# Half of the row squares moved to the head, the rest given two products to land, and row factors written to DRAM in runs

## The chip, the cores and the metric

The kernel runs on one core of one Trainium2 chip. The metric is the device time of one execution in microseconds (us). The core has five engines with queues of their own: TensorE (PE, with a separate unit for weight loads, PEld), VectorE (DVE), ScalarE (ACT), GpSimd (POOL) and SyncE (SP). Transfers (DMAs) are issued from the queues of SP, ACT and POOL and run on 16 shared DMA engines.

## The reference, cut to what matters

One layer of an encoder block is applied to two batches with shared weights, 512 and 256 tokens, together T = 768 rows of D = 2048 numbers in float32:

```
h = RMSNorm(x) * g;  z = h @ w_in           # columns: fourier 1024 | q 1024 | k 256 | v 256
of = fourier_mix(z fourier);  oa = windowed attention(q, k, v)
x = x + [RMSNorm(of) | RMSNorm(oa)] @ w_out
x = x + relu(RMSNorm(x) @ w_up)**2 @ w_down
y = RMSNorm(x)
```

RMSNorm needs one factor for each row of x, rsqrt(mean(x * x) + eps). The kernel does not scale x by it before the first product: it multiplies gains into x, computes z without the row factor, and applies the factor later to the columns of the transposed z (tile `rb`) or to the attention's probabilities (tile `r0`).

## The kernel before, in words

All large products are made of three float32r matmuls: each operand is split into a high part (a copy to float32r on ACT) and a low part (the rest, a subtraction on DVE), and high x high, high x low and low x high are summed in PSUM. So every operand costs one ACT and one DVE instruction ahead of PE.

The change lies in the first 170 us, which have three stages.

1. **The head** (inside the pool `xp`): x transposed is loaded by SP in chunks of one or two blocks of 128 of the 2048 columns (`chunks`, `load_x`), alternating with the weights of v (`load_wv`, four tiles `wv` with the tag `raw`). `prepare(c)` scales a chunk by the gains and splits it; `v_term` makes 36 matmuls of 256 columns for two blocks (line 425). The last chunk also makes the high and low parts of the first two weight pieces (`high7`, `low7`). Then come `xsum` (differences of x blocks on DVE) and `v_keep`, which copies the six results of v out of PSUM.
2. **The 28 products** (pool `hq`, the loop over n): the Fourier columns of z by a seven-product scheme (`names7`) with four weight pieces each. Iteration n issues, in the order of the code: x operand parts (`high_at`), the weight sums, `high7(n + 3)`, `low7(n + 2)`, further x parts (`low_at`), `product7(n)` (24 matmuls of 384 columns, line 276), the copy or addition of the results before (`out7`), and the load of the weights for n + 5. SP, ACT and DVE keep this written order, as PE does everywhere. Among the `low_at` steps are `first_load` and `first_split`, which fetch the first x block again into the tile `d7` and split it for the next stage.
3. **The rest of z** (line 789, 20 weight pieces), with the Fourier transform beside it; `fold` multiplies by `rb` at line 550.

The rows' squares stand in stage 2. From n = 10 on, POOL loads x by rows in 24 pieces of 512 numbers (`row_load`, line 482) into the tile `d7`, three at a time, and ACT squares and sums each in place (`row_square`, line 486) into one column of `ssq`. A piece can be loaded only when ACT is through with the one that was there. At n = 20 `row_norms` sums the columns (DVE), makes the factor `r0` [128, 6] (POOL, lines 98 and 101), writes it to DRAM (line 491) and reads it back as a row spread over all partitions, `rb` (line 492):

```
nc.gpsimd.dma_start(r0_d[0].rearrange("(m p) -> p m", p=P), r0[:])
nc.gpsimd.dma_start(rb[:], r0_d[0].partition_broadcast(P))
```

The tile pool `hq` uses the memory of `xp` after it; its weight tiles `wr` come first, as the tiles `raw` do in `xp`. PSUM has four buffers with the tag `ps` and four with `f`, shared by v, the products and the next stage.

Of the kernel before, what the change touches and what calls it, by code (L numbers as in the profile page):

```python
# [40 lines left out]
def hybrid_encoder(ctx: ExitStack, tc: tile.TileContext, a: dict):  # L41
# [83 lines left out]

    gall = cpool.tile([P, 3 * NK], F32, tag="gall", name="gall")
    g0, gm, gcat = (gall[:, i * NK : (i + 1) * NK] for i in range(3))
    r0_d = dpool.tile([1, T], F32, tag="r0d", name="r0d")
    ss0, r0, r1, r2, rm, ry = (stat(x) for x in ("ss0", "r0", "r1", "r2", "rm", "ry"))
    ssx, ssy = stat("ssx", NM * 4), stat("ssy", NM * 4)  # L130
    ssq = ssx

    def transpose4(ps, src):

# [62 lines left out]
    with ExitStack() as ph:  # L197
# [135 lines left out]

        def first_load(e):
            fx["d"] = hq["p"].tile([P, 4, HALF], F32, tag="d7", name="d7")[:]
            nc.sync.dma_start(fx["d"], a["x_t"][:, 0, 4 * e : 4 * e + 4, :])

        def first_split(e):
            for i in range(4):
# [26 lines left out]
            step(high_at, 20 + e, lambda e=e: xhigh(h0, b21, e))  # L366
            step(low_at, 20 + e, lambda e=e: xlow(l0, b21, h0, e))
        step(low_at, 22, first_block)
        step(low_at, 22, lambda: first_load(0))
        for e in range(2):  # L370
            step(low_at, 24 + 2 * e, lambda e=e: first_split(e))
            if e == 0:
# [3 lines left out]
        with tc.tile_pool(name="xp", bufs=1, reuse_waits="tile") as xp, tc.manual_schedule(  # L376
            engines={mybir.EngineType.SP, mybir.EngineType.Activation, mybir.EngineType.DVE}
        ):

            wv = [xp.tile([P, 4, 256], F32, tag="raw", name="raw", bufs=4) for _ in range(4)]  # L380
            whl = [[wpool.tile([P, 4, 256], F32R, tag=t, name=t, bufs=4) for t in ("wh", "wl")] for _ in range(4)]
            flat = xs[1][:].rearrange("p o k t -> p (o k t)").rearrange("p (s o t) -> p s o t", s=8, o=2)
            vt = xp.tile([P, 4, 2, HALF], F32R, tag="vt", name="vt")
            room = [flat[:, 0:4], flat[:, 4:8], vt[:]]
            chunks = [(0, 1), (1, 1), (2, 2), (4, 2), (6, 2), (8, 2), (10, 2), (12, 2), (14, 2)]
            homes = [(0, 0), (0, 1), (0, 2), (1, 0), (1, 2), (2, 0), (0, 0), (1, 0), (2, 0)]
            xhl = {}

            def load_x(k0, n):
                for t in range(2):  # L390
                    nc.sync.dma_start(xr[k0 // 8][t][:, k0 % 8 : k0 % 8 + n, :], a["x_t"][:, t, k0 : k0 + n, :])

            def load_wv(k0, n, queue=nc.sync):
                queue.dma_start(wv[k0 // 4][:, k0 % 4 : k0 % 4 + n, :], w_in[9][:, k0 : k0 + n, :])

            def prepare(c):

                k0, n = chunks[c]
                r, s0 = homes[c]
                ks = slice(k0 % 8, k0 % 8 + n)  # L400
                raw = [xr[k0 // 8][t][:, ks, :] for t in range(2)]
                rows = [room[r][:, s0 + i * n : s0 + i * n + n] for i in range(2 if k0 >= 8 else 1)]
                if k0 < 8:
                    parts = [[xs[0][:, o, ks, :] for o in range(2)]]
                else:
                    parts = []
                parts += [[x[:, :, o, :] for o in range(2)] for x in rows]
                xhl[c] = parts
                w, wk = k0 // 4, slice(k0 % 4, k0 % 4 + n)
                wh, wl = (x[:, wk, :] for x in whl[w])  # L410
                for i in range(n):
                    nc.scalar.activation(raw[0][:, i], raw[0][:, i], AF.Copy, scale=g0[:, k0 + i : k0 + i + 1])
                gb = g0[:, k0 : k0 + n].rearrange("p (k o) -> p k o", o=1).to_broadcast([P, n, HALF])
                nc.vector.tensor_tensor(out=raw[1], in0=raw[1], in1=gb, op=ALU.mult)
                split(wh, wl, wv[w][:, wk, :])
                for t in range(2):
                    split(*parts[t], raw[t])

            pv = [pp.tile([P, 512], F32, tag="f" if m < 4 else "ps", bufs=4, name="pv") for m in range(NM)]

            def v_term(c, m, term, i):
                k0, n = chunks[c]
                l, r = ((0, 0), (0, 1), (1, 0))[term]
                k = k0 + i
                nc.tensor.matmul(  # L425
                    pv[m][:, :256], xhl[c][m // 3][l][:, i, m % 3 * P : (m % 3 + 1) * P], whl[k // 4][r][:, k % 4, :],
                    start=(k == 0 and term == 0), stop=(k == NK - 1 and term == 2),
                )

            def v_keep(m):  # L430
                split(vhl[:, m, :, 0, :], vhl[:, m, :, 1, :], pv[m][:, :256].rearrange("p (g d) -> p g d", g=NKV))

            pw = pp.tile([P, 512], F32, tag="ps", bufs=4, name="pw")
            for i in range(9):
                nc.tensor.matmul(pw[:, :P], ones[:], ones[:], start=True, stop=True)
            nc.scalar.activation(mhalf[:, 7:8], mhalf[:, 7:8], AF.Copy)
            nc.scalar.dma_start(gall[:], a["gains"])
            load_wv(0, 1)
            load_x(*chunks[0])
            load_wv(1, 1)  # L440
            load_x(*chunks[1])
            load_wv(2, 2)
            load_x(*chunks[2])
            load_wv(4, 4)
            load_x(*chunks[3])
            load_x(*chunks[4])
            load_wv(8, 4)
            load_x(*chunks[5])
            load_x(*chunks[6])
            load_wv(12, 4)  # L450
            load_x(*chunks[7])
            load_x(*chunks[8])
            load7(0)
            load7(1)
            for c, (k0, n) in enumerate(chunks):
                prepare(c)
                if c == 5:
                    nc.scalar.dma_start(ident[:], a["c_ident"])
                if c + 1 < len(chunks):
                    for term in range(3):  # L460
                        for m in range(NM):
                            for i in range(n):
                                v_term(c, m, term, i)
                else:
                    for n2 in range(2):
                        high7(n2)
                        low7(n2)
                    for m in range(NM):
                        for term in range(3):
                            for i in range(n):  # L470
                                v_term(c, m, term, i)
            for n in range(2):
                xsum(b11, b12, b11, n)
            for m in range(NM):
                v_keep(m)

        def row_load(i):
            m, h = divmod(i, 4)
            if i == 0:
                raw7["x"] = hq["p"].tile([P, 4, HALF], F32, tag="d7", name="d7")[:].rearrange("p k t -> p (k t)")  # L480
            xt = raw7["x"][:, i % 3 * 512 : (i % 3 + 1) * 512]
            nc.gpsimd.dma_start(xt, x_rows(m)[:, h * 512 : (h + 1) * 512])  # L482
# [5 lines left out]
        def row_norms():  # L488
            nc.vector.tensor_reduce(out=ss0[:], in_=ssq[:].rearrange("p (m h) -> p m h", h=4), op=ALU.add, axis=AX.X)
            rsqrt_of(r0[:], ss0[:], D, NM, nc.gpsimd)  # L490
            nc.gpsimd.dma_start(r0_d[0].rearrange("(m p) -> p m", p=P), r0[:])
            nc.gpsimd.dma_start(rb[:], r0_d[0].partition_broadcast(P))

        with tc.tile_pool(name="hq", bufs=1, reuse_waits="tile") as hq["p"], tc.manual_schedule(
            engines={mybir.EngineType.SP, mybir.EngineType.Activation, mybir.EngineType.DVE}
        ):
            for n in range(2, 5):
                load7(n)
            high7(2)
            for n in range(NP7):  # L500
                for fn in high_at.get(n, ()):
                    fn()
                sum7(n + 3)
                high7(n + 3)
                low7(n + 2)
                for fn in low_at.get(n, ()):
                    fn()
                product7(n)
                out7(n - 1)
                load7(n + 5)  # L510
                if n == 10:
                    for i in range(3):
                        row_load(i)
                for i in range(3 * n - 36, 3 * n - 33):
                    if 0 <= i < 4 * NM:
                        row_square(i)
                for i in range(3 * n - 33, 3 * n - 30):
                    if 3 <= i < 4 * NM:
                        row_load(i)
                if n == 20:  # L520
                    row_norms()
            out7(NP7 - 1)
            out7(-1)

# [1291 lines left out]
```

## Time and profile before

| | |
|---|---|
| time, median of 3 runs | 2591.98 us (2587.20 to 2593.43) |
| the profiled execution | 2586.95 us, its span 2585.1 us |
| PE busy | 2565.6 us, 99% of the span |
| DVE, ACT, POOL busy | 1795.9, 1122.6, 252.9 us |
| mean granted clock of TensorE | 0.997 |

The span is the time between the first and the last instruction that the profiler shows. In the rows of a timeline stand the start, the duration, the engine, the line, the operation, the tiles written and read, and in brackets the idle time before it with what ended it. In the rows of waits stand who waited for whom, the us in total, how often, and the longest. In the rows of windows stand, for each stretch, the busy us of PE, PEld, DVE, ACT and POOL with their counts, the granted clock of TensorE, the busy share of the DMA engines and GB/s.

### The profile page before, as it was taken

Reading aid. Unit: us, or ns where it says so; the run is one execution under the profiler, and the core shown is the slowest. Engines: PE = TensorE matmul, PEld = TensorE weight load, DVE = VectorE, ACT = ScalarE, POOL = GpSimd, SP = SyncE. Lnnn points to the kernel's source line nnn. Section 1 sums busy time; section 2 is a strip of 40 time slices with the busy share of each in tenths; the row PEclk is TensorE's granted clock in tenths of the full one; section 3 lists DMA queues with packets and bytes.
Section 4 is the critical chain, followed back from the end, with each engine's and each line's share of the span. In section 5 each row is a group of like instructions: output and inputs, shape, how many; then the busy total and the mean of one; then the engine's idle time right before and its main releaser. Section 6 shows DMA issues by size and latency. Waiting matters only on the chain.

```text
span 2585.1 us, 34796 instructions
## 1 busy us (share of the span) xinstructions
PE 2565.6 (99%) x13462; PEld 2347.8 (91%) x13462; DVE 1795.9 (69%) x2212; ACT 1122.6 (43%) x1627; POOL 252.9 (10%) x355
## 2 busy tenths in 40 slices
PE   9999999999999999999999999999999999999998
PEld 9999998888899999999999999988888888888887
DVE  8756558787565555556777787667776766777687
ACT  6644337674333333334444544433333333333335
POOL 0112322222201011000000000110000000000000
PEclk9999999999999999999999999999999999999999
DMA  7673467455664445456666666775543662554364
GB/s 262 223 206 128 130 218 224 138 151 197 220 198 162 153 170 186 153 188 241 217 220 225 228 212 207 260 297 177 181 155 112 217 232 81 175 186 157 100 212 149
DMA packets 259479, 487.84 MB, mean 189 GB/s; under 512 B 20656, under 2 KB 147376, under 8 KB 259056
## 3 DMA queue, kind: packets, MB, share of 16 engines
q1 hardware_dynamic: 187104, 320.20, 38.7%
q10 hardware_dynamic: 58512, 112.05, 11.4%
q0 software_dynamic: 13696, 53.36, 6.0%
q8 instruction: 106, 1.74, 0.3%
q14 instruction: 61, 0.50, 0.1%
HBM read 365.99 MB, written 119.54 MB: 188 GB/s over the span
## 4 chain that ended last, share of the span: by engine, by line
PE 94%; DMA 2%; DVE 2%; issue 1%; ACT 1%; POOL 0%; SPq 0%; POOLq 0%; DVEq 0%; ACTq 0%
PE pu L1183 36%; PE pd L1618 35%; PE pm L1036 9%; PE pz L789 5%; PE p L276 2%; PE pv L425 1%; PE o L914 1%; PE s L835 1%; PE t L892 1%; PE ptx L136 0%; DMA d<-in_x_t 0%; PE pe L618 0%; POOL d L482 0%; PE pa L597 0%; DMA zf<-zf 0%
## 5 line engine op out<-in xcount | busy, mean ns | idle before, releaser
L1183 PE MATMUL pu<-xf,wh 128*128 128x384 f32 x3072 | 780.3, 334 | 0.0
L1183 PEld LDWEIGHTS pu<-xf,wh 128*128 128x128 f32 x3072 | 554.1, 188 | 1.5 <-ACT o L1201 1.3
L1618 PE MATMUL pd<-wh,sh 128*128 128x512 f32 x1332 | 517.7, 389 | 0.0
L1618 PE MATMUL pd<-wl,sh 128*128 128x512 f32 x1332 | 517.7, 389 | 0.0
L1618 PE MATMUL pd<-wh,sl 128*128 128x512 f32 x1332 | 517.5, 389 | 0.0
L1183 PE MATMUL pu<-xf,wl 128*128 128x384 f32 x1536 | 513.1, 334 | 0.0
L1595 ACT ACTIVATE wh<-rd 128x1024 fp32r<-128x1024 f32 x200 | 202.5, 1054 | 522.1 <-PE pd L1618 413.3
L1605 DVE TENSOR_TENSOR wl<-rd,wh 128x1024 fp32r<-128x1024 f32 x200 | 236.1, 1221 | 226.2 <-ACT wh L1595 225.5
L1163 ACT ACTIVATE wh<-ur 128x1024 fp32r<-128x1024 f32 x160 | 170.1, 1063 | 382.7 <-PE pu L1183 204.9
L1618 PEld LDWEIGHTS pd<-wh,sl 128*128 128x128 f32 x1332 | 249.9, 188 | 52.2 <-DVE sl L1606 0.3
L1618 PEld LDWEIGHTS pd<-wh,sh 128*128 128x128 f32 x1332 | 250.0, 188 | 51.7
L1618 PEld LDWEIGHTS pd<-wl,sh 128*128 128x128 f32 x1332 | 250.0, 188 | 51.7
L1183 PEld LDWEIGHTS pu<-xf,wl 128*128 128x128 f32 x1536 | 288.4, 188 | 0.0
L1169 DVE TENSOR_TENSOR wl<-ur,wh 128x1024 fp32r<-128x1024 f32 x160 | 195.5, 1222 | 76.1 <-ACT wh L1163 76.1
L1204 DVE TENSOR_TENSOR o<-pu,o 128x768 f32<-128x768 f32 x160 | 152.9, 956 | 122.5 <-PE pu L1183 114.9
L1588 DVE TENSOR_TENSOR rd<-rd 128x1024 f32<-128x1024 f32 x112 | 131.7, 1218 | 0.0
L1183 PE MATMUL pu<-xs,wh 128*128 128x384 f32 x512 | 129.9, 334 | 0.0
L1163 ACT ACTIVATE wh<-sx 128x1024 fp32r<-128x1024 f32 x64 | 67.9, 1062 | 130.5 <-PE pu L1183 104.4
L276 PE MATMUL p<-xs,wh 128*128 128x384 f32 x448 | 116.2, 340 | 4.1 <-DVE z L293 3.3
L1606 DVE TENSOR_TENSOR sl<-sr,sh 128x768 fp32r<-128x768 f32 x111 | 105.6, 951 | 0.0
L1169 DVE TENSOR_TENSOR wl<-sx,wh 128x1024 fp32r<-128x1024 f32 x64 | 78.2, 1223 | 23.8 <-ACT wh L1163 23.6
L1183 PEld LDWEIGHTS pu<-xs,wh 128*128 128x128 f32 x512 | 92.5, 188 | 0.0
(283 smaller groups left out, 3856.2 us busy)
## 6 DMA issues: line engine op xcount, KB each, us to landing
rd<-in_w_down SPq DMA_DIRECT2D x176, 512.0 KB, 4.9
ur<-in_w_up SPq DMA_DIRECT2D x128, 512.0 KB, 3.9
sr<-sd SPq DMA_DIRECT2D x95, 384.0 KB, 5.1
pd<-o ACTq DMA_DIRECT2D x60, 384.0 KB, 2.3
o<-pd POOLq DMA_DIRECT2D x60, 384.0 KB, 6.0
sd<-sm ACTq DMA_DIRECT2D x60, 384.0 KB, 2.7
raw<-in_w_in SPq DMA_DIRECT2D x42, 512.0 KB, 4.3
raw<-in_w_out SPq DMA_DIRECT2D x32, 512.0 KB, 4.5
```

Source lines behind the costliest of these rows:

```text
L276: nc.tensor.matmul(ps7[bank, g, r][:, :HALF], l[:, i, r * P : (r + 1) * P], x[:, o, 4 * e + i, :], start=(opens and e == 0 and i == 0 and ...
L789: nc.tensor.matmul(ps[c][s][:, :HALF], w[:, i, cs], whole[j // 2][s][o][:, 4 * (j % 2) + i, :], start=first and n == 0, stop=stop and n == 2,)
L1036: nc.tensor.matmul(ps, l(k), w[:, k % 2, :], start=(k == 0 and n == 0), stop=(k == 7 and n == 2))
L1163: nc.scalar.activation(wh[:], raw[:], AF.Copy)
L1169: nc.vector.tensor_tensor(out=wl[:], in0=raw[:], in1=f32(wh[:]), op=ALU.subtract)
L1183: nc.tensor.matmul(ps[:, t, :HALF], w[:, i, t * P : (t + 1) * P], xb[:, o, i, :], start=(s == first_of[bank] and i == 0 and n == 0), stop= ...
L1204: nc.vector.tensor_tensor(out=o, in0=src, in1=o, op=ALU.add)
L1588: add = lambda x, y, op: nc.vector.tensor_tensor(out=x[:], in0=x[:], in1=y[:], op=op)
L1595: nc.scalar.activation(wh[:], t[:], AF.Copy)
L1605: nc.vector.tensor_tensor(out=wl[:], in0=t[:], in1=f32(wh[:]), op=ALU.subtract)
L1606: nc.vector.tensor_tensor(out=sl[:], in0=sr[:], in1=f32(sh[:]), op=ALU.subtract)
L1618: nc.tensor.matmul(o, l[:, q, ts], w[:, ns], start=(j == j0 and (q, t) == (0, 0)), stop=(j == j1 and (q, t) == (1, 2)),)
```

## The change

- The head: the chunk of blocks 2 and 3 becomes two chunks of one block each, loaded in the order v weights, x, v weights, x.
- Rows 0 to 2 of the six blocks of rows are squared in the head, in six halves of 1024 numbers. POOL loads them into the tiles that held the v weights; ACT squares four ahead of the first high parts of weights and two behind them. The other 12 pieces of 512 stay in the loop: loads at n = 10, 12, 14 and 16, squares at n = 12, 14, 16 and 18. `ssq` is cleared at the start, since only two of its four columns are written for the first three blocks.
- `row_norms` moves from n = 20 to n = 18. At n = 21 PE transposes `r0` to [6, 128]; at n = 24 ACT copies that to SBUF, and POOL writes it to DRAM as six runs of 512 bytes and reads it back spread.
- `first_load` goes from SP's queue to POOL's, and its first call from step 22 to step 20.
- The identity for the transpose is loaded at n = 0, not in the head.

```diff
-    r0_d = dpool.tile([1, T], F32, tag="r0d", name="r0d")
+    r0_d = dpool.tile([NM, P], F32, tag="r0d", name="r0d")
...
+    nc.vector.memset(ssq[:], 0.0)
...
         def first_load(e):
             fx["d"] = hq["p"].tile([P, 4, HALF], F32, tag="d7", name="d7")[:]
-            nc.sync.dma_start(fx["d"], a["x_t"][:, 0, 4 * e : 4 * e + 4, :])
+            nc.gpsimd.dma_start(fx["d"], a["x_t"][:, 0, 4 * e : 4 * e + 4, :])
...
-        step(low_at, 22, lambda: first_load(0))
+        step(low_at, 20, lambda: first_load(0))
...
-            chunks = [(0, 1), (1, 1), (2, 2), (4, 2), (6, 2), (8, 2), (10, 2), (12, 2), (14, 2)]
-            homes = [(0, 0), (0, 1), (0, 2), (1, 0), (1, 2), (2, 0), (0, 0), (1, 0), (2, 0)]
+            chunks = [(0, 1), (1, 1), (2, 1), (3, 1), (4, 2), (6, 2), (8, 2), (10, 2), (12, 2), (14, 2)]
+            homes = [(0, 0), (0, 1), (0, 2), (0, 3), (1, 0), (1, 2), (2, 0), (0, 0), (1, 0), (2, 0)]
...
+            def half_load(i):
+                m, h = divmod(i, 2)
+                halves[i] = xp.tile([P, 4, 256], F32, tag="raw", name="xt", bufs=4)[:].rearrange("p a b -> p (a b)")
+                nc.gpsimd.dma_start(halves[i], x_rows(m)[:, h * 1024 : (h + 1) * 1024])
+
+            def half_square(i):
+                m, h = divmod(i, 2)
+                nc.scalar.activation(halves[i], halves[i], AF.Square, accum_out=ssq[:, 4 * m + h : 4 * m + h + 1])
...
             for c, (k0, n) in enumerate(chunks):
                 prepare(c)
-                if c == 5:
-                    nc.scalar.dma_start(ident[:], a["c_ident"])
+                for i in {6: (0, 1), 8: (2,), 9: (3, 4, 5)}.get(c, ()):
+                    half_load(i)
...
+                    for i in range(4):
+                        half_square(i)
                     for n2 in range(2):
                         high7(n2)
                         low7(n2)
+                    for i in range(4, 6):
+                        half_square(i)
...
-            nc.gpsimd.dma_start(r0_d[0].rearrange("(m p) -> p m", p=P), r0[:])
-            nc.gpsimd.dma_start(rb[:], r0_d[0].partition_broadcast(P))
+
+        def row_turn():
+            pr = raw7["r"] = pp.tile([P, 512], F32, tag="ps", bufs=4, name="pr0")
+            nc.tensor.transpose(pr[:NM, :P], r0[:], ident[:])
+
+        def row_spread():
+            pr = raw7.pop("r")
+            nc.scalar.copy(rb[:NM, :P], pr[:NM, :P])
+            nc.gpsimd.dma_start(r0_d[:], rb[:NM, :P])
+            nc.gpsimd.dma_start(rb[:], r0_d[:].rearrange("m p -> (m p)").partition_broadcast(P))
...
-                if n == 10:
-                    for i in range(3):
+                if n == 0:
+                    nc.scalar.dma_start(ident[:], a["c_ident"])
+                if n in (12, 14, 16, 18):
+                    for i in range(3 * n // 2 - 6, 3 * n // 2 - 3):
+                        row_square(i)
+                if n in (10, 12, 14, 16):
+                    for i in range(3 * n // 2 - 3, 3 * n // 2):
                         row_load(i)
-                for i in range(3 * n - 36, 3 * n - 33):
-                    if 0 <= i < 4 * NM:
-                        row_square(i)
-                for i in range(3 * n - 33, 3 * n - 30):
-                    if 3 <= i < 4 * NM:
-                        row_load(i)
-                if n == 20:
+                if n == 18:
                     row_norms()
+                if n == 21:
+                    row_turn()
+                if n == 24:
+                    row_spread()
```

More of the change, by code (lines that the diff above doesn't have):

```diff
@@ L428, in v_term @@
                 )
+            def half_load(i):
[5 more added lines that the diff above has]
+                nc.scalar.activation(halves[i], halves[i], AF.Square, accum_out=ssq[:, 4 * m + h : 4 * m + h + 1])
+            halves = {}
             def v_keep(m):
@@ L437, in hybrid_encoder @@
             nc.scalar.dma_start(gall[:], a["gains"])
[L438 to L452, printed above, removed]
+            for c in range(4):
+                load_wv(c, 1)
+                load_x(*chunks[c])
+            for c in range(4, 10, 2):
+                load_wv(2 * c - 4, 4)
+                load_x(*chunks[c])
+                load_x(*chunks[c + 1])
             load7(0)
@@ L478, in row_load @@
             m, h = divmod(i, 4)
-            if i == 0:
+            if i == 12:
                 raw7["x"] = hq["p"].tile([P, 4, HALF], F32, tag="d7", name="d7")[:].rearrange("p k t -> p (k t)")
```

## The prediction, made before the changed kernel had run

> **What bounds the kernel now.** I read the page's head and chain first, then who TensorE (PE) waits for, then the clock by windows, then the timeline of the engines where PE waits.
>
> ```profile
> span 2585.1 us, 34796 instructions
> PE 2565.6 (99%) x13462; PEld 2347.8 (91%) x13462; DVE 1795.9 (69%) x2212; ACT 1122.6 (43%) x1627; POOL 252.9 (10%) x355
> ...
> PE p L276 <- DVE z L293: 3.3, 1, 3.3
> PE pv L425 <- ACT xs L69: 1.9, 1, 1.9
> PE p L276 <- DVE wl L261: 1.5, 1, 1.5
> ...
> PE p L276 <- ACT wh L253: 0.8, 1, 0.8
> ...
> 117.20:123.90 6.70, 3.40 (x13) 3.11 (x12) 5.41 (x6) 6.66 (x11) 2.15 (x4) 0.75 0.55 166
> 143.30:151.30 8.00, 5.74 (x22) 5.10 (x22) 7.73 (x8) 6.06 (x8) 4.95 (x3) 0.79 0.66 225
> ...
> 12.16 30.51 PE pv L425 x252
> 42.67 49.77 PE p L276 x287
> ...
> 42.51 0.51 PE L276 MATMUL p<-xs,wh 128*128 128x384 f32 x2
> ...
> 120.86 0.98 PE L276 MATMUL p<-xs,wh 128*128 128x384 f32 x2 [3.30 <-DVE z L293]
> ...
> 168.51 0.34 PE L276 MATMUL p<-xs,wl 128*128 128x384 f32 x1
> 169.48 1.17 PE L789 MATMUL pz<-xf,wh 128*128 128x384 f32 x4 [0.63 <-ACT wh L69]
> ```
>
> PE is busy 99% of the span, so only its few holes can be won; all named ones lie before 170 us. The last number but two of a window row is the granted clock: beside both holes it is 0.75 and 0.79, so a hole costs its width and a slow stretch behind it. The two waits before the second hole, 0.8 and 1.5, and the first, 3.3, are 5.6 us of width. How much in all: unhindered, 287 matmuls of the 28 products (line 276) take 49.77 us, 0.1734 each. The products hold 28 x 24 = 672, thus 116.5 us; they run from 42.51 to 168.68 (the last starts at 168.51), 126.2 us. So **9.7 us are lost inside the products**, of which the clock behind the holes is 9.7 - 5.6, about 2 each; 0.6 more at the entry to the next stage and 1.9 in the head.
>
> Who makes the two holes? The row squares on ScalarE (ACT), whose order is fixed:
>
> ```profile
> 86.63 1.81 POOL L482 DMA_DIRECT2D d<-in_x_prompt  x3 [86.20 <-DVE xs L313]
> ...
> 94.22 0.63 ACT L486 ACTIVATE d<-d 128x512 f32<-128x512 f32 x1
> ...
> 110.05 0.54 POOL L482 DMA_DIRECT2D d<-in_x_prompt  x1 [1.01 <-ACT d L486]
> ...
> 114.27 0.63 ACT L486 ACTIVATE d<-d 128x512 f32<-128x512 f32 x1 [3.56 <-DMA d<-in_x_prompt]
> ...
> 116.99 1.47 ACT L310 ACTIVATE xs<-xr 128x1536 fp32r<-128x1536 f32 x1
> ...
> 118.49 1.76 DVE L313 TENSOR_TENSOR xs<-xr,xs 128x1536 fp32r<-128x1536 f32 x1 [6.52 <-ACT xs L310]
> ...
> 141.34 0.63 ACT L486 ACTIVATE d<-d 128x512 f32<-128x512 f32 x1 [0.34 <-DMA d<-in_x_sample]
> ...
> 143.35 1.04 ACT L253 ACTIVATE wh<-raw 128x1024 fp32r<-128x1024 f32 x1
> ...
> DMA to landing us min/median/max: 3.0/6.0/7.4
> ```
>
> A batch of three loads lands 3.0 to 7.4 us after its issue, but its squares stand one product later, 24 x 0.1734 = 4.16 us. ACT waits at 114.27; behind it stand the split of an x operand (line 310) and VectorE's low half, done at 120.25, just before PE resumes at 120.86. Before the second hole a weight's high part (143.35) stands behind the squares of 141.34. Where a batch had two products, 86.63 to 94.22, no wait is marked.
>
> **The change part by part.** All sums are against the profiled execution, 2586.95 us (span 2585.1 and 1.85 around it). That is 5.0 below the median of the runs, 2591.98, so the forecast for the median is the same difference taken from 2591.98.
>
> *Squares with two products to land.* Only rows 3 to 5 stay in the products: loads at n = 10, 12, 14, 16, squares at 12 to 18. Two products are 8.3 us against 7.4 for the slowest landing. Each batch can only be issued when ACT has squared the one before in the same tile (as at 110.05), some 2 us into its iteration, so ACT may still wait about 1 us; the weights it splits are for a product three ahead, 12 us. Both holes go, with their slow clock: all of the 9.7, unless something else is late. Next late is VectorE's low half, which had 4 us in hand (below).
>
> *Loads of the first x block from POOL instead of SP, at step 20.* SP had waited for the squares there, with weight loads behind it; it now issues those freely.
>
> ```profile
> SPq L336 <- ACT d L486: 8.6, 1, 8.6
> ```
>
> On POOL the load stands behind the two row-norm operations, which take 4 us behind the squares of n = 18 (42.5 + 18 x 4.16 = 117.4, and ACT's own work up to about 121), so to 125, and its data are needed from n = 24, at 142. The second load follows the first split, near 147, and at the 7.4 of the slowest row load lands by 155; PE gets there at 159. Zero, with 4 us to spare.
>
> *The row factors.*
>
> ```profile
> 145.43 1.09 POOL L98 TENSOR_SCALAR r<-ss 128x6 f32<-128x6 f32 x1 [10.54 <-DVE ss L489]
> 146.60 2.93 POOL L101 TENSOR_TENSOR r<-r,mhalf 128x6 f32<-128x6 f32 x1
> ...
> r0d<-r POOLq DMA_DIRECT2D x1, 3.0 KB, 11.3
> ...
> 183.45 0.97 DVE zf L550
> ...
> L892 PE MATMUL t<-ident,p x224: 270/272/281, 386.8 to 579.5; 128*128 128x128 f32 x112
> ```
>
> The 3 KB write of 768 single floats took 11.3 us; six runs of 512 B should land in about 3. Its reader is the product with rb at 183.45, 14 us behind the entry to the stage; that the chain gets shorter is worth nothing itself. What it may have cost is the 0.6 at the entry, where a weight load came late beside it. I take half, 0.3, between 0 and 0.6. Added: one transpose on PE, 0.27 (its clean-up copy on ACT about 0.3, hidden by ACT's idle time), and a new wait: PE, in order, stands behind the power on POOL. The norms are ready at about 125 and the transpose stands after product 21, at 42.5 + 22 x 4.16 = 134, so 9 us spare.
>
> *The head, chunks.*
>
> ```profile
> 3.59 0.61 ACT L412 ACTIVATE xr<-xr,gall 128x384 f32<-128x384 f32 x1 [1.37 <-DMA xr<-in_x_t]
> ...
> 6.21 0.62 ACT L412 ACTIVATE xr<-xr,gall 128x384 f32<-128x384 f32 x1 [0.68 <-DMA xr<-in_x_t]
> ...
> 9.73 1.12 ACT L412 ACTIVATE xr<-xr,gall 128x384 f32<-128x384 f32 x2 [1.52 <-DMA xr<-in_x_t]
> ...
> 14.45 1.56 ACT L69 ACTIVATE xs<-xr 128x768 fp32r<-128x768 f32 x2
> ...
> 5.00:10.00 5.00, 4.96 (x35) 4.40 (x36) 3.08 (x7) 2.66 (x6) 0.00 (x0) 1.00 0.94 311
> 10.00:12.00 2.00, 0.30 (x3) 0.10 (x1) 1.33 (x2) 2.00 (x4) 0.00 (x0) 1.00 1.01 372
> ...
> DMA to landing us min/median/max: 2.4/7.5/9.0
> ```
>
> Chunk 2 of two blocks becomes two of one, to close the 1.9 us hole at 12.16. Its first half can start as chunk 1 ends. But the DMA engines are full here (0.94, 1.01) and move 311 GB/s of small pieces against 372 of larger ones: 1.05 MB take 3.4 us against 2.8, 0.6 later; by the landings (2.6 us a one-block chunk: chunk 0 at 3.59, chunk 1 at 6.21) up to 5.3 against 3.5, 1.8 later. The following chunk's operand was ready at 14.45 + 0.8 = 15.2 and PE took it at 12.16 + 36 x 0.121 = 16.5, so it had 1.3 in hand. PE then stands at 16.5 - 0.7 to 16.5 + 0.5: a gain of 0.7 to a loss of 0.5. I take 0.
>
> The Trainium skill, "DMA: Bandwidth & Descriptors", section Bandwidth, speaks against it: batch to 1 MiB or more, since each DMA pays a fixed 2.0 us. By it, an estimate, three more DMAs cost 6.0 us, 4.7 beyond the 1.3, and the whole change would give 5 us. The trace does not show them paid one after the other.
>
> The rows' own end of that: if each of the three added DMAs cost a whole shortest landing of line 391, 2.4, the head would lose 7.2 - 1.3 = 5.9. Against it, three DMAs of chunk 1 land within 2.6 us of chunk 0.
>
> *The head, half rows.*
>
> ```profile
> 30.80 0.68 DVE L70 TENSOR_TENSOR wl<-raw,wh 128x512 fp32r<-128x512 f32 x1
> ...
> 39.11 0.38 ACT L69 ACTIVATE vhl<-pv 128x256 fp32r<-128x256 f32 x1 [5.39 <-PE pv L425]
> ...
> 53.59 1.22 DVE L261 TENSOR_TENSOR wl<-ws,wh 128x1024 fp32r<-128x1024 f32 x1
> ...
> 30.00:34.00 4.00, 4.00 (x36) 4.00 (x35) 4.00 (x6) 3.62 (x5) 0.00 (x0) 1.00 0.03 8
> ```
>
> Six loads of 512 KB on POOL (half i is 1024 columns of row block i // 2) into the value weights' buffers, and six squares, each about 1.0 + 0.2 us (the 1024-wide copy at 143.35 takes 1.04). Four stand ahead of the first weights' high parts. The fourth load must wait for the last value weights' low half (31.5) and the new chunk's extra instructions (about 0.7), so 32.2. DMA engines are idle then (0.03). Bounds: 3.0, the fastest half-sized load, to 14.8, twice the slowest; I take 4.3, near the low end since the engines are free. It lands at 36.5, is squared by 37.7; the high parts end at 39.7, the low ones by 41: PE needs them at 42.5, so nothing is lost until the landing passes 39.3. ACT then squares halves 4 and 5 (issued when halves 0 and 1 are squared, near 33.7 and 35, landing 38 and 39.5) and reaches the value copies at 42 instead of 39.11, and VectorE, with its x sum ahead of them, ends them near 46.5 instead of 43.5. The weight loads for product 2 go into the same memory, so SP waits for those squares too (about 41, landing 45; product 2 starts at 50.8). VectorE's low part for product 4 moves from 54.8 to about 57.5, and PE needs it at 42.5 + 4 x 4.16 = 59.1. So 1.6 us remain, and the price is 0.
>
> **Sum**: -9.7 holes and clock, -0.3 entry, +0.3 transpose, 0 head: **-9.7 us**: 2577.3 in the profiled execution's terms, 2582.3 in the median's. Bounds: -11 with head and entry gains; -6 with 3 us lost in the head.
>
> **The rivals.**
>
> *Half rows late* (small gain). For: the loads are twice the size, share engines that are full until 30 us, and everything has only 1.6 to 2.8 us in hand. Against: engines idle at 30 to 34. If half 3 lands at 41 and half 5 at 46, product 0 waits 1.6 for its low part, the value copies end near 49.7, products 2 and 4 wait another 1, and one slow stretch adds 2: 4.6 us lost, -5 in all, 2587.
>
> *Small pieces late* (small gain): the 5.9 above leaves -4, 2588. The skill's rule would give -5, an estimate.
>
> *The squares block the first products* (slower). If half 3 takes twice the slowest row load, 14.8, it lands at 47, and halves 4 and 5, 7.4 apart behind it, at 54 and 62. Product 0 waits 7; the copies end near 65.5, product 2's low part at 66.7 instead of before 50.8, 9 more; two slow stretches add 4: 20 lost, +10, 2602. It decides from half 5 landing at about 53, where the loss equals the 9.7. Against: twice the size need not take twice the time when the fastest row load took 3.0.
>
> *The change doesn't do it:* ACT still waits in the products, since each batch waits for the squares before. With 1 to 2 us of wait in each of three batches and 12 us in hand, no hole; if one stays, half is won: 2587.
>
> **How the numbers follow.** Likeliest 0.66 (2576 to 2586); half rows late 0.17; small pieces late 0.03; one hole stays 0.08; slower 0.06. What a measurement can tell from no change is 0.3%, 7.8 us. The likeliest's -9.7 lies only 2 beyond it, so a tenth of its weight falls within: faster 0.60, same 0.34, slower 0.06. Runs of the kernel before alone spread over 6 us (2587.2 to 2593.4), which widens all. Range 2575 to 2591: it takes in the late cases and the profiled level less 11.
>
> **What would show it.** Right: no wait of line 276 on VectorE or ACT past 100 us, clock 1.00 from 42 to 160; stage line 789 starting at 159 to 160; the DRAM write of row factors landing in 3 us. Head right: half 3 landing before 39, no PE wait between 12 and 60. Wrong: PE waits of line 276 at 42 to 60 on lines 253 or 261, squares waiting for their loads in the head, or a wait at the transpose near 134.

## The result, and the profile after

| | before | after |
|---|---|---|
| median of 5 runs | 2591.40 us (2587.20 to 2593.43) | 2577.34 us (2575.98 to 2578.38) |
| the profiled execution | 2586.95 us, span 2585.1 | 2578.38 us, span 2576.6 |

The ratio is 0.9947, 95% interval 0.9933 to 0.9962: 14.1 us by the medians, 8.6 us between the two profiled executions. The forecast was 2582.3, in a range of 2575 to 2591. The median came out 5.0 lower than the forecast, and where that 5.0 comes from is a question of the experiments. Line numbers move a little: 276 becomes 277, 425 becomes 426, 486 becomes 494, 789 becomes 808.

First the page's head of the changed kernel, and who TensorE waits for in the first 200 us (us in total, how often, the longest):

```profile
span 2576.6 us, 34801 instructions
PE 2562.9 (99%) x13463; PEld 2346.1 (91%) x13463; DVE 1796.0 (70%) x2217; ACT 1120.6 (43%) x1619; POOL 249.0 (10%) x351
...
PE pv L426 <- ACT xs L69: 3.0, 2, 2.3
PE pw L447 <- DVE ssx L132: 1.0, 1, 1.0
```

The four waits of lines 276 and 789 are gone: no product and not the entry to line 808 waits any more. The chain of the work that ended last (start, duration, engine, line) shows what that is worth:

```profile
16.86 27.68 PE pv L426 x216
44.55 91.53 PE p L277 x528
136.08 0.11 PE pr L502
136.19 24.97 PE p L277 x144
161.15 9.01 PE pz L808 x52
```

The 672 matmuls take 91.53 + 24.97 = 116.50 us, which is what 672 unhindered ones were worked out to take; before, 126.2. From the products' start to the entry it is 161.15 - 44.55 = 116.6 us against 169.48 - 42.67 = 126.8, a gain of 10.2. But the products start at 44.55 instead of 42.67, a loss of 1.9. Together 8.3 of the 8.5 by which the span is shorter; behind 161 the two kernels do the same.

PE's row at its wait in the head and the windows (busy us of PE, PEld, DVE, ACT, POOL, then granted clock, DMA share, GB/s) show where the 1.9 went, and that the clock is whole where the holes were:

```profile
16.86 1.41 PE L426 MATMUL pv<-wh,xs 128*128 128x256 f32 x8 [2.25 <-ACT xs L69]
...
16.00:18.00 2.00, 1.14 (x8) 1.14 (x9) 2.00 (x4) 2.00 (x5) 0.00 (x0) 0.94 1.03 413
18.00:20.00 2.00, 2.00 (x12) 2.00 (x11) 1.58 (x3) 1.81 (x4) 0.00 (x0) 0.50 1.02 408
20.00:22.00 2.00, 2.00 (x14) 2.00 (x14) 2.00 (x4) 0.84 (x1) 0.54 (x1) 0.70 1.04 421
...
110.00:120.00 10.00, 10.00 (x60) 10.00 (x59) 7.53 (x7) 7.17 (x12) 1.61 (x3) 1.00 0.81 246
140.00:150.00 10.00, 10.00 (x60) 10.00 (x59) 5.74 (x9) 5.35 (x8) 1.18 (x2) 1.00 0.37 109
```

PE's wait of 2.25 us in the head (line 426, for the chunk of blocks 4 and 5, which it starts at 16.86) is followed by half the clock from about 18 on: 12 and 14 matmuls in two microseconds instead of 19.

ScalarE still waits for row pieces, and it no longer matters:

```profile
105.41 0.63 ACT L494 ACTIVATE d<-d 128x512 f32<-128x512 f32 x1 [1.65 <-DMA d<-in_x_prompt]
...
115.43 0.64 ACT L494 ACTIVATE d<-d 128x512 f32<-128x512 f32 x1 [2.46 <-DMA d<-in_x_sample]
```

### The profile page after: what moved, and what is told of

Same layout as the page of the kernel before. It is cut to its first block, busy times and chain, and to the rows that moved or that the text cites. A ratio compares the mean times of both kernels' runs of the same rounds, so it can differ in the third digit from the quotient of the medians.

```text
span 2576.6 us, 34801 instructions
## 1 busy us (share of the span) xinstructions
PE 2562.9 (99%) x13463; PEld 2346.1 (91%) x13463; DVE 1796.0 (70%) x2217; ACT 1120.6 (43%) x1619; POOL 249.0 (10%) x351
## 4 chain that ended last, share of the span: by engine, by line
PE 94%; DVE 2%; DMA 1%; ACT 1%; issue 1%; POOL 0%; SPq 0%; ACTq 0%; DVEq 0%; POOLq 0%
PE pu L1202 36%; PE pd L1637 35%; PE pm L1055 8%; PE pz L808 6%; PE p L277 5%; PE pv L426 1%; PE o L933 1%; PE t L911 1%; PE s L854 1%; DVE p L869 0%; PE pe L637 0%; DMA xr<-in_x_t 0%; PE pa L616 0%; PE ptx L137 0%; DMA oar<-oad 0%
```

## The experiments

The theory ahead of the runs was that of the prediction: the squares make the holes, their pace removes them. Open were the 5.0 us by which the median beat the forecast, and the 1.9 us lost in the head. "Before" runs beside the experiments had medians of 2589.70 to 2591.03.

**No squares in the loop at all.** The kernel before, without its row loads and squares; the factors come from a constant, so that part of the computation is left out.

```diff
-                if n == 10: ... row_load(i)
-                ... row_square(i) ... row_load(i)
+    nc.vector.memset(ssq[:], 1.0)     # at the start
```

> The kernel before with its 24 row loads and squares of the product loop left out (the row factors are then made from a constant). Theory 1 (the row squares at one product's time make both holes in the products and the slow clock behind them): no wait of the products on VectorE or ScalarE past 100 us, products in 116.5 to 117.5 us instead of 126.2, the span 9.5 to 10.5 us shorter than before. Rival (the holes come from weight loads or from the first-block load on SP): at least one hole of over 1 us stays and the span is less than 6 us shorter.

Measured: 2576.07 us, ratio 0.9945 (0.993 to 0.996). The chain:

```profile
12.34 31.98 PE pv L426 x252
44.32 116.48 PE p L277 x672
```

Without squares the products run in 116.48 us without a wait. So the squares and their loads, which this run leaves out together, make both holes, and no arrangement of them can win more than the 9.7 there. The median falls by more, 14.8: with no squares to wait for, POOL issues the old write of the factors at 131.21 instead of 149.82, and PE does not wait at the entry to the next stage either. The changed kernel is within its spread of a kernel that has no squares.

**The old chunks.** The changed kernel with blocks 2 and 3 in one chunk and the old order of loads.

```diff
-            chunks = [(0, 1), (1, 1), (2, 1), (3, 1), (4, 2), ...
+            chunks = [(0, 1), (1, 1), (2, 2), (4, 2), ...
```

> The changed kernel with the head's chunk of blocks 2 and 3 in one piece again, in the old order of loads; all else as changed. Theory A (small pieces land late: the two one-block chunks put the next chunk's x 1.5 us later, PE waits 2.25 us for it and loses 1.7 us more to a halved clock): the products start near 42.6 instead of 44.4, the clock stays at 1.00 from 10 to 30 us, span 1.5 to 2.0 us shorter than the changed kernel's 2576.6. Rival B (the half-row load that POOL issues at 12.2 us beside the x loads makes them late): the products still start at 44 or later and the span stays within 0.7 us of 2576.6.

Measured: 2577.91 us (2575.57 to 2578.63), ratio 0.9949 (0.9935 to 0.9964). PE's row at its wait in the head, the chain and two windows:

```profile
12.83 1.92 PE L426 MATMUL pv<-wh,xs 128*128 128x256 f32 x12 [2.23 <-ACT xs L69]
...
12.83 32.02 PE pv L426 x252
44.84 91.53 PE p L277 x528
...
14.00:16.00 2.00, 2.00 (x12) 2.00 (x11) 1.54 (x3) 1.84 (x4) 0.00 (x0) 0.54 1.02 413
16.00:18.00 2.00, 2.00 (x13) 2.00 (x12) 2.00 (x4) 2.00 (x4) 0.00 (x0) 0.61 1.04 424
```

The small pieces are not what makes the start late: with the old chunks the wait is as long (2.23), the clock drops as deep, and the products start later still. The split is worth nothing measurable in either direction. The 2 us for each DMA that the prediction took from the Trainium skill, "DMA: Bandwidth & Descriptors", stand there in the section Anatomy of one DMA, for DMAs that GpSimd issues. For the three more DMAs here, which SP issues, no such cost shows.

**The turn alone.** The kernel before, squares as they were, with the factors turned by PE's transpose at n = 23 and the write in runs at n = 25.

```diff
-            nc.gpsimd.dma_start(r0_d[0].rearrange("(m p) -> p m", p=P), r0[:])
-            nc.gpsimd.dma_start(rb[:], r0_d[0].partition_broadcast(P))
+                if n == 23: row_turn()
+                if n == 25: row_spread()
```

> The kernel before with the row factors turned by PE (at n = 23) and written in runs, nothing else changed. Prediction's step: the DRAM write lands in about 2 to 3 us instead of 11.3, the 0.6 us at the entry to line 789 shrinks by 0 to 0.6, both holes stay: span 0 to 0.6 us shorter than before. Rival (the slow write delays much else in the DMA engines): over 1.5 us shorter.

Measured: 2585.59 us (2583.43 to 2587.19, 10 runs) against 2590.88, ratio 0.9979 (0.997 to 0.9989): 5.3 us, by the interval 2.9 to 7.8. PE's waits from 100 to 180, and the entry in the timeline (line 801 here):

```profile
PE p L276 <- DVE z L293: 3.3, 1, 3.3
PE p L276 <- ACT wh L253: 2.6, 1, 2.6
PE p L276 <- DVE wl L261: 1.4, 1, 1.4
...
169.84 0.85 PE L801 MATMUL pz<-xf,wh 128*128 128x384 f32 x4
```

Both product holes stay, the wait at the entry goes. The prediction gave the entry 0.3, between 0 and 0.6; in the median even the lower end of the interval is far above that. So most executions of the kernel before must lose more by the write than the 0.63 at the entry of its profile. That is concluded from the medians: the two profiled executions differ by only 0.9 (span 2584.2 against 2585.1). The next run shows one execution that does lose more.

The edit changes the form of the write and also its place, 158.93 instead of 149.82. That the form counts is seen beside it: while the six runs were written, from 159.0 to 164.5, the DMA engines moved 368 GB/s; in the kernel before, beside the single floats, they moved 59 from 150.5 to 161.0, with the loads for the next stage issued at 151.54, 155.90 and 157.96 under way.

**The kernel before, profiled again.**

> The kernel before once more, for its profile. The profiled execution of before (2586.95 us) lies 4.5 us under the median of its runs (2591.4). If the holes vary in width with the landing of the row loads and with the clock behind them, the products' stretch differs from 126.2 us by what the time differs from 2586.95; if the stretch is 126.2 again while the time is near 2591, the spread lies elsewhere.

Measured: 2589.93 us, span 2588.1. PE's first row of the next stage, ScalarE's two waits ahead of it, and two windows:

```profile
171.54 1.17 PE L789 MATMUL pz<-xf,wh 128*128 128x384 f32 x4 [3.70 <-DVE z L293]
...
165.49 1.06 ACT L69 ACTIVATE wh<-raw 128x1024 fp32r<-128x1024 f32 x1 [10.96 <-DMA raw<-in_w_in]
168.08 2.13 ACT L72 ACTIVATE xf<-d,gall 128x384 fp32r<-128x384 f32 x4 [1.53 <-DMA d<-in_x_t]
...
150.00:160.00 10.00, 10.00 (x59) 10.00 (x59) 7.41 (x12) 3.09 (x5) 1.04 (x2) 1.00 0.71 62
170.00:180.00 10.00, 8.46 (x38) 8.27 (x39) 6.38 (x9) 3.38 (x4) 0.00 (x0) 0.83 0.68 229
```

The same in the first profile of the kernel before:

```profile
164.29 1.06 ACT L69 ACTIVATE wh<-raw 128x1024 fp32r<-128x1024 f32 x1 [9.14 <-DMA raw<-in_w_in]
...
150.00:160.00 10.00, 10.00 (x56) 10.00 (x55) 6.91 (x10) 3.09 (x5) 0.75 (x1) 0.95 0.73 62
```

In the second profile the entry costs 3.70 us and a clock of 0.83 behind it (1.7 us in ten), where the first had 0.63 and no drop: a third hole like the other two. Read it from the DMA columns: while the write of 768 single floats is under way (issued at 150.41, read back from 162.61), the engines are 0.71 busy and move 62 GB/s. The weight load issued at 152.12 takes 13.3 us to land and the x load issued at 155.37 takes 12.7, so both land only behind the write, and ScalarE has waited 10.96 for the weights. VectorE's low parts wait for ScalarE; behind them, from 170.85, stands the addition of line 293 that PE waits for. In the first profile the window reads 0.73 and 62, and ScalarE waited 9.14: nearly the same delay, which just fitted.

The expectation asked whether the holes inside the products make the spread between executions. They do not: the products took 125.0 us here against 126.2, in a span that is 3.0 longer.

**The old write, but early.** The changed kernel without the transpose, the single floats written straight behind the norms.

```diff
             rsqrt_of(r0[:], ss0[:], D, NM, nc.gpsimd)
+            nc.gpsimd.dma_start(r0_d[0].rearrange("(m p) -> p m", p=P), r0[:])
...
-                if n == 21: row_turn()        # and row_spread keeps only the read
```

> The changed kernel with the old form of the row factors' write: 768 single floats straight from r0, issued on POOL behind the norms at n = 18, no transpose; the spread read stays at n = 24. Theory 'the entry only has to find the write gone': the write, issued near 130, takes 11 to 12 us as before, lands near 142, 19 us ahead of the entry at 161; its slow packets delay only weight loads that have four products in hand. Time as the changed kernel, 2576 to 2579, no wait at line 808's first matmul. Rival 'single floats cost wherever they stand': the 5 us that the turn alone was worth come back, as a wait of PE between 130 and 165: 2581 to 2583.

Measured: 2576.70 us, ratio 0.9947 (0.9932 to 0.9962). The DMA row (KB, us to landing), POOL's timeline and the chain:

```profile
r0d<-r POOLq DMA_DIRECT2D x1, 3.0 KB, 11.7
...
129.06 0.93 POOL L499 DMA_DIRECT2D r0d<-r  x1 [0.30 <-POOL r L101]
141.01 0.57 POOL L506 DMA_DIRECT2D rb<-r0d  x1 [11.02 <-DMA r0d<-r]
...
42.84 116.48 PE p L277 x672
159.32 12.48 PE pz L804 x72
```

The write is as slow as ever, 11.7 us, and costs nothing, since it is through 18 us ahead of the entry. The turn and the earlier norms are two cures of one wait: the turn alone takes some 5 us from the kernel before, and where the norms come earlier, leaving the turn out costs nothing.

**The old pace with half the pieces.** The changed kernel with squares at n = 12, 13, 14, 15.

```diff
-                if n in (12, 14, 16, 18):
-                    for i in range(3 * n // 2 - 6, 3 * n // 2 - 3):
+                if n in (12, 13, 14, 15):
+                    for i in range(3 * n - 24, 3 * n - 21):
                         row_square(i)
-                if n in (10, 12, 14, 16):
+                if n in (10, 12, 13, 14):     # three pieces each
```

> The changed kernel with its 12 remaining pieces in the loop at the old pace: squares at n = 12, 13, 14, 15 (loads at 10, 12, 13, 14), so one product between a load and its square. Theory 'the pace made the holes': ACT waits 1 to 3.5 us in each of the batches of n = 13, 14 and 15, and line 277 waits on DVE or ACT between 100 and 125, a hole of 2 to 3 us with about 2 of slow clock behind it: 2580 to 2583. Rival 'the number of batches in a row made them': the first hole of the kernel before came after three batches, the second after six; with three batches behind the first, the 12 us by which the splits run ahead absorb their waits and no hole comes: 2576 to 2579.

Measured: 2589.47 us (2587.47 to 2592.14, 10 runs), ratio 0.9999 (0.999 to 1.0008): the whole gain is gone. ACT, DVE and PE in the timeline, then a window behind the hole:

```profile
116.79 0.63 ACT L494 ACTIVATE d<-d 128x512 f32<-128x512 f32 x1 [4.00 <-DMA d<-in_x_sample]
119.58 0.63 ACT L494 ACTIVATE d<-d 128x512 f32<-128x512 f32 x1 [2.07 <-DMA d<-in_x_sample]
121.08 1.47 ACT L311 ACTIVATE xs<-xr 128x1536 fp32r<-128x1536 f32 x1
...
122.57 1.76 DVE L314 TENSOR_TENSOR xs<-xr,xs 128x1536 fp32r<-128x1536 f32 x1 [8.53 <-ACT xs L311]
124.25 1.01 DVE L294 TENSOR_TENSOR z<-p,z 128x384 f32<-128x384 f32 x2
...
124.95 0.98 PE L277 MATMUL p<-xs,wh 128*128 128x384 f32 x2 [7.56 <-ACT xs L311]
...
125.00:130.00 5.00, 5.00 (x16) 5.00 (x17) 5.00 (x5) 2.44 (x2) 0.00 (x0) 0.50 0.52 167
```

One hole of 7.56 us, then 16 matmuls in 5 us where 29 fit. The rows give the chain that the prediction had not followed to its end. The late square holds ScalarE's high part of an x operand (121.08); VectorE's low part waits for that (122.57); behind it, in VectorE's written order, stands the addition that takes the result before out of PSUM (line 294, 124.25); and the product that accumulates in that bank waits for the addition. The trace names ScalarE as PE's releaser because its instruction of 123.40 ended last; by the code that one is for group 5 of the products, and product 18, which begins here, belongs to group 4, whose bank the additions free. PE resumes when the first of the two is through. ScalarE waited 4.00 and 2.07 us for the pieces of this batch, and PE stood for 7.56: the three products by which weights are split ahead did not cover it. I expected 2 to 3 us of hole; the rival, that a short row of batches is absorbed, fell altogether.

The transpose cost something here too: PE waited 2.2 us at it for the factors, which POOL delivered only at 146.5. So not all of the loss is the pace's; the hole and the slow clock behind it are about 9.8 us of it (7.56, and 13 matmuls of 0.17 that are missing in the five microseconds behind).

**The head, three ways.** Seven unused matmuls in PE's wait; the first two half loads held back until the chunk at place 5 is prepared (a small write to their tile, in VectorE's written order, for which the load has to wait); both.

```diff
+                    if c == 3:
+                        for i in range(7):
+                            nc.tensor.matmul(pw[:, :P], ones[:], ones[:], start=True, stop=True)
...
+                if i == 0:                        # the loads (0, 1) after prepare(5), on their old engine
+                    nc.vector.memset(halves[i][:, :1], 0.0)
```

> The changed kernel with seven unused matmuls (ones by ones into pw, about 0.2 us each at full clock) on PE behind the fourth chunk of the head, where PE waits 2.2 us for the fifth. Theory 'the clock drop is what made the head 1.9 us later': the idle time shrinks to under 1 us, the clock stays at 1.00 from 16 to 22, the products start 1.5 to 2 us earlier, at 42.4 to 42.9, and the median is 2575 to 2576. Rival 'the drop has another cause or the fifth chunk is late by itself': clock 0.5 again behind it, products at 44 or later, 2577 to 2579.

> The changed kernel with the first two half loads of POOL held back until the sixth chunk is prepared (they were issued near 12, among the head's own loads). Theory 'the half loads share the DMA engines and make the fifth chunk late': PE's wait for it falls from 2.25 to 1.9 or less, no clock drop, products start at 42.5 to 43, 2575 to 2576. Rival 'they do not matter there': the wait stays at 2.1 to 2.3 with the drop behind it, as in the two kernels whose fourth and fifth pieces differ and in one without half loads; 2577 to 2579.

> The changed kernel with both edits to its head: seven unused matmuls in PE's wait for the fifth chunk, and the first two half loads held back. Theory 'what the head still loses is a wait of 1.5 to 2.2 us and sometimes a clock drop of about 1.6 behind it': the clock stays at 1.00, the products start at 42.3 to 42.9, the median is 2575 to 2577, within 1 us of each edit alone. Rival 'the two gains add': 2574 to 2575.

Measured: 2577.06, 2576.59 and 2577.15 us, ratios 0.9949, 0.9948 and 0.9946, each interval about 0.0013 either way. The chain of the first:

```profile
16.81 26.20 PE pv L426 x216
43.00 91.53 PE p L277 x528
```

In all three profiles the clock stays at 1.00 and the products start at 43.00, 42.55 and 42.04, up to 2.5 us earlier. The same 216 matmuls take 26.20 instead of 27.68, so a clock drop costs 1.5. The medians do not fall with it: the three stand within 0.8 us of the changed kernel, whose own runs span 2.4. The early write's profile (above) had no drop either and a span 0.2 longer than the changed kernel's; it lost 2.1 later, in one wait of the attention:

```profile
PE s L850 <- DVE mx L865: 2.1, 1, 2.1
```

From the first matmul behind the products to the end of the span, where no edit of these runs stands, the 13 profiles take 2413.2 to 2417.6 us: that scatter of 4.4 is more than the head's 1.5 to 2.5. For the timed runs, which have no profile, where the head's gain goes stays open. Nor did the held-back loads settle the cause of PE's wait (of the two, one had been issued at 12.24, the other only at 20.99): the wait fell to 1.36 with them, but it was 1.46 in the early write's profile, without. None of these versions beats the changed kernel by more than its spread.

**Half rows and pace alone.** The changed kernel with the old chunks and the old write (behind the norms at n = 18) at once, and then also with the first x block's load back on SP at step 22.

> The changed kernel with two of its parts undone at once: the chunk of blocks 2 and 3 is one again with the old order of loads, and the row factors are written in the old form behind the norms at n = 18 and read back at n = 24. Left of the change: half rows in the head, two products for each batch, the first x block's load on POOL. Theory 'the squares' place and pace are the whole gain': 2576 to 2579, products in 116.5 us without a wait, no wait at the entry. Rival 'each part undone alone is covered by the other': 2 us or more are lost, by a wait at the entry or in the head: 2580 to 2583.

> As the run e9_pace_only, and the first x block is again loaded from SP's queue, at step 22. Theory 'the queue does not matter once the squares are through before it': the last squares end near 125, SP's load is issued near 133, its data are needed from 142: 2576 to 2579. Rival 'SP with weight loads behind it is late': SP waits at line 336 of old for the tile, the weight loads of the entry come late and PE waits 1 to 4 us at the entry to line 808: 2578 to 2583.

Measured: 2576.09 us, ratio 0.9948 (0.9934 to 0.9961), and 2577.45 us, 0.9949 (0.9937 to 0.9962). The chain of the first:

```profile
12.63 30.51 PE pv L426 x252
43.14 116.48 PE p L277 x672
159.62 12.48 PE pz L812 x72
```

What is left of the change in the second run is the half rows in the head, two products for each batch, the norms at n = 18 with the read-back at n = 24, and the identity loaded later. That is the whole gain, both the holes and the entry. Half rows without the pace gained nothing (2589.47, above); the pace without the half rows was not run, and its eight batches would need 16 products.

## Why the prediction was right, and where its steps were not

- **Holes in the products, -9.7:** right to a tenth, 126.2 to 116.5 us, and for the reason given. The cover it named, "three ahead, 12 us", was wrong: the old pace shows that lateness reaches PE through the addition out of PSUM, when ScalarE waits 4.00 and 2.07 in one batch. What holds is that two products leave less to wait: 1.65 and 2.46 at most, and no hole at PE.
- **Entry, -0.3 (0 to 0.6): the mis-sized term.** It was bounded by one profiled execution that happened to show 0.63. In the median the write costs about 5, by the turn alone (5.3, interval 2.9 to 7.8). The prediction carried the 5.0 by which that execution lies below the median over to the forecast as a constant; the turn alone says that most of it belonged to the change. -9.7 and -5.3 make -15.0, with a loss of up to 1.9 in the head -13.1 to -15.0, and -14.1 was measured. That the median still fell in the range is owed to its lower end, which was drawn from the level of the profiled execution; the sum's own bound of -11 is 2581 in the median's terms.
- **The head, chunks, 0 (gain 0.7 to loss 0.5):** the split is worth 0, as said, but the profiled loss, 1.9, lies outside the bounds. They had only the wait in them, not the half clock behind it, though the prediction counted just that for the other holes. Two of its signs failed by this: PE did wait between 12 and 60, and the next stage began at 161.15 instead of 159 to 160.
- **Half rows, 0:** held. Half 3 was squared from 38.36, after ScalarE had waited 0.58 for it; the forecast landing was 36.5, the limit 39.3, with PE itself 1.9 later. The value copies started at 43.78 (42), VectorE's low part for product 4 ended at 59.76 (57.5), and no product waited. The rival "half rows late" fell by about a microsecond.

```profile
38.36 1.06 ACT L438 ACTIVATE xt<-xt 128x1024 f32<-128x1024 f32 x1 [0.58 <-DMA xt<-in_x_prompt]
...
58.54 1.22 DVE L262 TENSOR_TENSOR wl<-ws,wh 128x1024 fp32r<-128x1024 f32 x1
```

- **Transpose, +0.3:** 0.11 on the chain, no wait; the factors were ready at 129, the transpose stood at 136.08. "The chain gets shorter is worth nothing itself" was right, the write in runs landed in 2.1 us (forecast 3), and by then it mattered to nobody.
- **First x block on POOL, 0:** right; the second load, issued at 148.51, let ScalarE start at 155.25, the 155 forecast. SP would have done as well.
- **One hole stays, 2587:** did not come, but its price, half of the 9.7, was too low: at the old pace half of the pieces made one hole of about 9.8 with its slow clock, and with the wait at the transpose the whole gain was gone.

## What to carry to other kernels

When a profile is 5 us below the median of the runs, profile the same kernel again before carrying the difference over: a transfer that only just fits in one execution can be a hole in another. Follow a late instruction along each engine's written order to the next thing that frees a buffer; the cover of one consumer says nothing of the one queued behind it. Before turning a slow write into a fast one, see whether it can start earlier: early enough, its 11.7 us cost nothing.

## What the runs showed of the hardware

**The clock drops after short waits, and not always.** In the head, waits of 1.36 to 1.85 us were never followed by a drop (six profiles); 2.09, 2.14, 2.23 and 2.25 were; 2.10 once was not. A drop is to 0.50 and cost 1.5 (27.68 against 26.20; 31.98, 32.01 and 32.02 against 30.51). It lasts about 3.4 us, worked out from the windows: in the changed kernel 0.06, 0.50 and 0.30 of the clock are missing in three stretches of 2 us, 1.7 us together, at half the clock. The Trainium skill, "TensorE: Matmul & The Clock Gate", Part 1, speaks of an idle window of about 3.4 us that runs free of the kernel; the halving and its length agree, a chance near the border would fit a free-running window, which no run here tests. But here 2.1 us without work were enough.

**A write of 3 KB can hold up the loads.** As 768 single floats it took 11.3 to 13.9 us in six profiles, and in the two of the kernel before it kept the DMA engines 0.71 and 0.73 busy at 62 GB/s; as six runs it took 1.7 to 5.4. The Trainium skill, "DMA: Bandwidth & Descriptors", in its rules for kernel authors, says that a strided last dimension becomes one descriptor per element; the trace adds that others' loads can wait behind it, a weight load 13.3 us beside the single floats, 5.9 beside the six runs of the turn alone.

**A small POOL instruction can be held for twelve microseconds.** In the run at the old pace:

```profile
133.15 1.22 DVE L246 TENSOR_TENSOR wr<-wr,ws 128x1024 f32<-128x1024 f32 x1
...
144.96 1.01 DVE L294 TENSOR_TENSOR z<-p,z 128x384 f32<-128x384 f32 x2
...
133.33 11.77 POOL L98 TENSOR_SCALAR r<-ss 128x6 f32<-128x6 f32 x1 [11.33 <-DVE ss L497]
```

The same instruction on 128 by 6 numbers took 0.43 in the changed kernel. From 133.15 VectorE ran nine instructions without a gap, each with both operands in SBUF; POOL's ended at 145.10, just after VectorE had come to one that reads PSUM. The Trainium skill, "SBUF — State Buffer", section Who interferes with whom, says that a VectorE instruction with two SBUF inputs contends with a GpSimd instruction that reads SBUF; its summary of rules adds that the later one blocks. These rows agree. So in this run a step on POOL's path to PE, which the transpose had made of the factors, depended on the gaps of VectorE.
